# Part of the next expert's gate product moved between an expert's up and down products, token transposes moved into up, and three paddings

## The chip, the cores and the metric

The kernel runs on one core of a Trainium2 chip. The metric is the device time of one execution in microseconds. Lower is better.

## The reference, cut to what matters

One encoder layer: an adaLN-modulated norm, one input projection into an attention group and an mLSTM group, an output projection, and then a mixture of 16 experts in which each expert picks its own 128 of the 1024 tokens. The change lies in the experts, and its paddings also move operands of the two projections.

```python
aff = jax.nn.softmax((h @ w_router).astype(jnp.float32), axis=-1)
gates, idx = lax.top_k(jnp.swapaxes(aff, 1, 2), cap)          # cap = 128 tokens of each expert
xe = jax.vmap(lambda hb, ib: hb[ib])(h, idx)
hid = jax.nn.silu(jnp.einsum('becd,edf->becf', xe, w_gate)) * jnp.einsum('becd,edf->becf', xe, w_up)
ye = jnp.einsum('becf,efd->becd', hid, w_down) * gates[..., None]
out = segment_sum(ye at idx)                                   # added into the residual stream
```

D is 2048 and the hidden width of an expert is 1024, in float32: each expert reads 8 MiB of gate, 8 MiB of up and 8 MiB of down weights.

## The kernel before

Every float32 product is made of three matmuls of a reduced float32 type (`mm3`, L416 to L418): high by high, high by low and low by high, where `hi` is the rounded operand and `lo` the rest. One matmul is 128x128 by 128x512.

**Weights of the experts.** They come in 384 chunks of 1 MiB through a ring of 14 slots (plus a few lent ones at the start); `load_next` (L921) issues one DMA on SP's queue (L941), and is called when a chunk has been split. A chunk holds two k, where a k is 128 rows of contraction by 1024 columns. `chunk` (L1312) splits each k: ScalarE writes `ehi` (L1321, 4 buffers), VectorE writes `elo` (L1327, 3 buffers). A k feeds 6 matmuls: 3 into each of two banks. Gate, up and down have 16 k each, so 96 matmuls each; a chunk column `cc` is 512 rows, that is 4 k in two halves.

**One expert.** `prep(e+1)` (L1256) makes the one-hot matrix of the next expert's tokens (`oh`, VectorE), 16 small matmuls for indices and gates, and issues the gather of its tokens on POOL's queue (L1268); ScalarE then scales the gathered rows (L1280). `gate_up(e)` (L1332) runs gate into two `acc` banks and up into two others; ScalarE applies Silu into the tile `y` (L1355, one buffer), and after up VectorE multiplies (L1359). `hidden_T` (L1363) transposes the hidden rows on TensorE (L1369), ScalarE and VectorE split them into `hT` (L1372, L1373). `tokens_T(e+1)` (L1284) transposes the next expert's tokens: 4 quarters of 4 transposes (L1293), each followed by four scalings into `xtmp` (L1302) and a split into `xh` and `xl` (L1305, L1306); xh and xl have one buffer for each quarter. `down(e)` (L1378) runs two halves of 1024 columns, both in the same two `s` banks; after each half VectorE scales them into `y` (L1394), and at the end an indirect DMA on POOL's queue adds `y` into the output (L1396).

**Order.** Engines take instructions in the order in which a scheduler placed them at build time by its own timeline; `tc.issue_after` adds an order on one engine. In the order before, up of expert e ends, 8 token transposes, 8 hidden transposes and 8 more token transposes follow, and then down.

**PSUM.** Four `acc` banks, two `s`, two `t`.

**Places in SBUF.** Tiles are laid one after the other. In the layout before, `quad1`, `quad2` and `quad3` (pool `big`, the split activations of the projections, L184) begin 128 bytes past a multiple of 256, as `y` and `hT` do; the other quads and the split weights `w_hi` and `w_lo` (pool `wp`) begin at a multiple of 256; `xh`, `xl`, `ehi` and `elo` begin 192 bytes past one. In the input projection (`block_T` L425, `block_N` L456) the first half of the contraction reads quads 0 to 3, the second half quads 4 to 7; in the output projection (`out_block` L758) the stationary operand is always in quads 1 to 4.

Of the kernel before, what the change touches and what calls it, by code (L numbers as in the profile page):

```python
# [19 lines left out]
D = 2048  # L20
# [64 lines left out]
def tile_kernel(ctx: ExitStack, tc: tile.TileContext, x, c, w_ada, b_ada, w_in, b_gates, q_gain, k_gain, sink,  # L85
# [829 lines left out]
    ew = ctx.enter_context(tc.tile_pool(name="ew", bufs=8, side="right"))  # L915
    chunks, left, extra = {}, [], []

    def order(e, i):
        return MIXED if e + i // 4 == 0 else PLAIN

    def load_next(eng=nc.sync):  # L921

        n = len(chunks)
        if n == 16 * 24:
            return
        n, slot = FIRST[n] if n < len(FIRST) else (n, (n - len(FIRST)) % RING)
        i, half = divmod(n, 2)
        e, i = divmod(i, 12)
        if i < 8:
            cc, half = order(e, i)[2 * (i % 4) + half]  # L930
            i += cc - i % 4
            src, off, ld = (w_gate, w_up)[i // 4], e * D * 1024 + (i % 4) * 512 * 1024, 1024
        else:
            src, off, ld = w_down, e * 1024 * D + (i % 2) * 512 * D + ((i - 8) // 2) * 1024, D
# [242 lines left out]
    mo_p = ctx.enter_context(tc.tile_pool(name="moe", bufs=1))  # L1177
    borrowed(mo_p, "y")
    borrowed(mo_p, "hT")
    mo_p.tile([128, 8], F32, name="pad")  # L1180
    while len(chunks) < len(FIRST):
        load_next()
    todo, made = [0], [0]
# [97 lines left out]
        p.update(mt=mt, idx=idx, xg=xg)  # L1281
        yield

    def tokens_T(p, after=None):  # L1284
        p["xh"], p["xl"], p["tmp"] = [], [], []
        for q in range(4):
            xh = mo_p.tile([128, 4, 128], F32R, name=f"xh{q}")
            xl = mo_p.tile([128, 4, 128], F32R, name=f"xl{q}")
            ps = bank("t")
            tmp = mo_p.tile([128, 512], F32, name="xtmp", bufs=2)  # L1290
            with tc.issue_after(after.ins) if after else nullcontext():
                for b in range(4):
                    nc.tensor.transpose(ps[:, b * 128:(b + 1) * 128],  # L1293
                                        p["xg"][:, (4 * q + b) * 128:(4 * q + b + 1) * 128], ident)
            for b in range(4):
                k = 4 * q + b
                bs = slice(b * 128, (b + 1) * 128)
                if after is None and b % 2:
# [12 lines left out]

    def chunk(half, direct=False):  # L1312
            raw = chunks[todo[0]]
            todo[0] += 1
            for j in range(2):
                if direct:
                    yield 2 * half + j, raw[:, j], None
                    continue
                hi = mo_p.tile([128, 1024], F32R, name="ehi", bufs=4)
                lo = mo_p.tile([128, 1024], F32R, name="elo", bufs=NLO)  # L1320
                nc.scalar.copy(hi, raw[:, j])  # L1321
                n = made[0]
                made[0] += 1
                r = min(int((n - NLO) * PACES), len(chain) - 1)
                wait = P[0]["at"] if n < NLO else chain[r] if n < 48 else None
                with tc.issue_after(wait.ins) if wait else nullcontext():
                    nc.vector.tensor_sub(lo, raw[:, j], hi)  # L1327
                yield 2 * half + j, hi, lo
            if todo[0] - 1 not in lent:
                load_next()  # L1330

    def gate_up(e, p, side):  # L1332
        accs = []
        for w in range(2):
            acc = [bank("acc") for _ in range(2)]
            last = order(e, 4 * w)[-1]
            for cc, half in order(e, 4 * w):

                direct = e == 0 and (w, cc) in DIRECT
                for j, hi, lo in chunk(half, direct):  # L1340
                    k = 4 * cc + j
                    for q in range(2):
                        qs = slice(q * 512, (q + 1) * 512)
                        if direct:
                            p["last"] = nc.tensor.matmul(acc[q], p["tmp"][cc][:, j * 128:(j + 1) * 128], hi[:, qs],
                                                         start=k == 0, stop=(cc, half) == last and j % 2 == 1)
                            continue
                        p["last"] = mm3(acc[q], p["xh"][cc][:, j], p["xl"][cc][:, j], hi[:, qs], lo[:, qs],
                                        k == 0, (cc, half) == last and j % 2 == 1)
                    side.step()  # L1350
            if w == 0:
                yt = mo_p.tile([128, D], F32, name="y", tag="y")
                sg = [yt[:, q * 512:(q + 1) * 512] for q in range(2)]
                for q in range(2):
                    nc.scalar.activation(sg[q], acc[q], AF.Silu)  # L1355
        p["y"], p["hid"] = yt, []
        for q in range(2):
            hid = yt[:, 1024 + q * 512:1024 + (q + 1) * 512]
            nc.vector.tensor_mul(hid.rearrange("t (j p) -> t p j", j=4), acc[q].rearrange("t (p j) -> t p j", j=4),  # L1359
                                 sg[q].rearrange("t (p j) -> t p j", j=4))  # L1360
            p["hid"].append(hid)

    def hidden_T(p):  # L1363
# [11 lines left out]
            p["hl"].append(hl)  # L1375
            yield

    def down(p, side):  # L1378
# [4 lines left out]
        for half in range(2):  # L1383
            acc = [bank("s") for _ in range(2)]
            for cc in range(2):
                for j, hi, lo in (s for half in range(2) for s in chunk(half)):
                    for q in range(2):
                        qs = slice(q * 512, (q + 1) * 512)
                        mm3(acc[q], p["hh"][cc][:, j], p["hl"][cc][:, j], hi[:, qs], lo[:, qs],
                            cc + j == 0, cc == 1 and j == 3)  # L1390
                    side.step()
            for q in range(2):
                qs = slice(half * 1024 + q * 512, half * 1024 + (q + 1) * 512)
# [5 lines left out]
    P, g2b = [{} for _ in range(16)], []  # L1399
# [4 lines left out]
    first.add(tokens_T(P[0]))  # L1404
    first.drain()
    run(select(tp))
    for e in range(16):
        if e < 15:
            side.add(prep(e + 1, P[e + 1]))
        gate_up(e, P[e], side)  # L1410
        side.drain()
        if e + 1 < 16:
            side.add(tokens_T(P[e + 1], P[e]["last"]))
        ht = hidden_T(P[e])
        side.step()
        next(ht)
        side.step()
        next(ht)
        down(P[e], side)
        side.drain()  # L1420


# [43 lines left out]
```

## Time and profile before

| | |
|---|---|
| median of 3 runs | 2886.38 us (2884.27 to 2890.02) |
| the profiled execution | 2886.07 us, its span 2884.4 us |
| busy: TensorE / its weight loads / VectorE / ScalarE / GpSimd | 93% / 74% / 74% / 54% / 13% |
| mean granted TensorE clock | 0.976 |
| moved by DMA | 744.34 MB, 258 GB/s over the span |

The experts run from about 1620 us to the end. In a row of a view, PE is TensorE, PEld its weight loads, DVE VectorE, ACT ScalarE, POOL GpSimd and SP the engine whose queue loads the weights; L416 is line 416 of the kernel; out<-in names tiles. Matmuls are pipelined, and a row's duration is longer than the distance from one to the next: the pace is read from start times, or from a window divided by the number of matmuls that start in it.

### The profile page before, as it was taken

Reading aid. Unit: us, or ns where it says so; the run is one execution under the profiler, and the core shown is the slowest. Engines: PE = TensorE matmul, PEld = TensorE weight load, DVE = VectorE, ACT = ScalarE, POOL = GpSimd, SP = SyncE. Lnnn points to the kernel's source line nnn. Section 1 sums busy time; section 2 is a strip of 40 time slices with the busy share of each in tenths; the row PEclk is TensorE's granted clock in tenths of the full one; section 3 lists DMA queues with packets and bytes.
Section 4 is the critical chain, followed back from the end, with each engine's and each line's share of the span. In section 5 each row is a group of like instructions: output and inputs, shape, how many; then the busy total and the mean of one; then the engine's idle time right before and its main releaser. Section 6 shows DMA issues by size and latency. Waiting matters only on the chain. (4 is left out here: it accounts for less than half of the span.)

```text
span 2884.4 us, 36984 instructions
## 1 busy us (share of the span) xinstructions
PE 2669.0 (93%) x12384; PEld 2137.3 (74%) x12384; DVE 2127.7 (74%) x3504; ACT 1571.8 (54%) x2585; POOL 370.7 (13%) x306
## 2 busy tenths in 40 slices
PE   6997999999999999999999697999999999999997
PEld 6786787777777787777888476777777777777776
DVE  7777767766656556666646787988888888888886
ACT  5222432334333324333545376887788887777775
POOL 0001222000000003333435310010000000000000
PEclk9998999999999999999999799999999999999999
DMA  8874426655555556565786588999999999999993
GB/s 294 281 247 119 151 79 200 189 171 191 172 169 188 161 174 230 211 204 179 278 290 206 197 289 313 365 347 364 370 362 360 361 360 363 351 351 354 358 339 135
DMA packets 269399, 744.34 MB, mean 258 GB/s; under 512 B 29197, under 2 KB 83209, under 8 KB 232217
## 3 DMA queue, kind: packets, MB, share of 16 engines
q1 hardware_dynamic: 249240, 684.37, 66.2%
q0 software_dynamic: 4768, 33.62, 4.5%
q10 hardware_dynamic: 15200, 24.00, 2.3%
q8 instruction: 97, 1.59, 0.2%
q14 instruction: 94, 0.76, 0.1%
HBM read 672.01 MB, written 69.90 MB: 257 GB/s over the span
## 5 line engine op out<-in xcount | busy, mean ns | idle before, releaser
L1327 DVE TENSOR_TENSOR elo<-ew,ehi 128x1024 fp32r<-128x1024 f32 x432 | 513.2, 1221 | 68.4 <-ACT ehi L1321 19.9
L1321 ACT CAST ehi<-ew 128x1024 fp32r<-128x1024 f32 x432 | 445.1, 1055 | 134.9 <-PE acc L418 71.6
L1327 DVE TENSOR_TENSOR elo<-quad,ehi 128x1024 fp32r<-128x1024 f32 x324 | 384.3, 1221 | 65.1 <-ACT ehi L1321 32.8
L417 PE MATMUL acc<-elo,xh 128*128 128x512 f32 x1008 | 395.7, 393 | 4.1 <-DVE elo L1327 4.0
L418 PE MATMUL acc<-ehi,xl 128*128 128x512 f32 x1008 | 393.5, 391 | 0.0
L1321 ACT CAST ehi<-quad 128x1024 fp32r<-128x1024 f32 x324 | 333.2, 1055 | 101.0 <-PE acc L418 51.1
L416 PE MATMUL acc<-quad,w_hi 128*128 128x512 f32 x896 | 362.9, 406 | 7.2 <-ACT w_hi L385 5.0
L418 PE MATMUL acc<-quad,w_lo 128*128 128x512 f32 x896 | 358.1, 402 | 2.8 <-DVE w_lo L386 2.8
L417 PE MATMUL acc<-quad,w_hi 128*128 128x512 f32 x896 | 359.8, 402 | 0.0
L206 DVE SCALAR_TENSOR_TENSOR ada_acc<-ada_w,csil,ada_acc 128x512 f32<-128x512 f32 x360 | 273.4, 760 | 83.7 <-DMA ada_w<-in_w_ada_dram 80.1
L385 ACT ACTIVATE w_hi<-w_raw,sc1p 128x128 fp32r<-128x128 f32 (+2 forms) x368 | 161.7, 490 | 318.0 <-PE acc L417 175.8
L416 PE MATMUL acc<-ehi,xh 128*128 128x512 f32 x1008 | 314.1, 393 | 10.8 <-ACT ehi L1321 10.8
L417 PE MATMUL acc<-w_lo,quad 128*128 128x512 f32 x768 | 313.3, 408 | 6.7 <-DVE w_lo L375 5.2
L418 PE MATMUL acc<-w_hi,quad 128*128 128x512 f32 x768 | 308.0, 401 | 0.0
L416 PE MATMUL acc<-w_hi,quad 128*128 128x512 f32 x768 | 298.8, 417 | 9.0 <-ACT ev L728 4.6
L769 POOL TENSOR_TENSOR w_raw<-w_raw,quad 128x512 f32<-128x512 f32 x136 | 184.4, 1366 | 899.5 <-DMA quad<-mod_d 612.0
L416 PEld LDWEIGHTS acc<-ehi,xh 128*128 128x128 f32 x1008 | 189.9, 189 | 52.2 <-ACT ehi L1321 11.7
L417 PEld LDWEIGHTS acc<-elo,xh 128*128 128x128 f32 x1008 | 190.1, 189 | 50.4 <-DVE elo L1327 9.9
L386 DVE SCALAR_TENSOR_TENSOR w_lo<-w_raw,sc1p,w_hi 128x128 fp32r<-128x128 f32 (+2 forms) x368 | 174.0, 502 | 69.9 <-ACT w_hi L385 67.7
L417 PE MATMUL s<-elo,hT 128*128 128x512 f32 x512 | 208.2, 407 | 15.9 <-DVE elo L1327 15.6
L418 PEld LDWEIGHTS acc<-ehi,xl 128*128 128x128 f32 x1008 | 190.0, 188 | 39.1
L416 PE MATMUL s<-ehi,hT 128*128 128x512 f32 x512 | 181.3, 405 | 38.9 <-DVE y L1394 19.5
(377 smaller groups left out, 4158.1 us busy)
## 6 DMA issues: line engine op xcount, KB each, us to landing
ada_w<-in_w_ada_dram SPq DMA_DIRECT2D x192, 512.0 KB
ew<-in_w_down_dram SPq DMA_DIRECT2D x74, 1024.0 KB
ew<-in_w_up_dram SPq DMA_DIRECT2D x73, 1024.0 KB
ew<-in_w_gate_dram SPq DMA_DIRECT2D x72, 1024.0 KB
quad<-in_w_up_dram SPq DMA_DIRECT2D x54, 1024.0 KB
quad<-in_w_down_dram SPq DMA_DIRECT2D x54, 1024.0 KB
quad<-in_w_gate_dram SPq DMA_DIRECT2D x54, 1024.0 KB
w_raw<-in_w_in_dram SPq DMA_DIRECT2D x176, 256.0 KB
```

What stands on the lines that cost most here:

```text
L206: alu.scalar_tensor_tensor(acc, t[:, j], csil[:, k:k + 1], acc, op0=OP.mult, op1=OP.add)
L385: nc.scalar.mul(h, r, s)
L386: nc.vector.scalar_tensor_tensor(l, r, s, h, op0=OP.mult, op1=OP.subtract)
L416: nc.tensor.matmul(ps, ah, bh, start=start, stop=False)
L417: nc.tensor.matmul(ps, ah, bl, start=False, stop=False)
L418: return nc.tensor.matmul(ps, al, bh, start=False, stop=stop)
L769: nc.gpsimd.tensor_mul(raw[:, 0], raw[:, 0], g1b[:, nb * 512:(nb + 1) * 512])
L1321: nc.scalar.copy(hi, raw[:, j])
L1327: nc.vector.tensor_sub(lo, raw[:, j], hi)
```

## The change

Between up and down of experts 1 to 14 stand the first 512 rows of contraction (chunk column 0, two halves of two k) of the next expert's gate product: one half, then the hidden transposes and the last quarter of the token transposes, then the other half. The first three quarters of the token transposes stand inside up, each after the last use of the xh and xl that it overwrites. The second half of down uses `acc` banks in place of the `s` banks. The list `uses` gives the loads the new order of use. Expert 0 keeps the old order. Three paddings grow: 128 bytes in `consts`, 128 in `mixconsts`, 192 in the pool of the experts, so that all operands named above begin at a multiple of 256 bytes.

```diff
+    consts.tile([128, 32], F32, name="pad")
...
-    mc.tile([128, 8], F32, name="pad")
+    mc.tile([128, 40], F32, name="pad")
...
-    def order(e, i):
-        return MIXED if e + i // 4 == 0 else PLAIN
+    def order(e, w):
+        return MIXED if e + w == 0 else PLAIN
+    uses = []
+    for e in range(16):
+        uses += [(e, 0, cc, half) for cc, half in order(e, 0) if e < 2 or cc]
+        uses += [(e, 1, cc, half) for cc, half in order(e, 1)]
+        if 0 < e < 15:
+            uses += [(e + 1, 0, 0, half) for half in range(2)]
+        uses += [(e, 2 + part, cc, half) for part in range(2) for cc in range(2) for half in range(2)]
...
-    mo_p.tile([128, 8], F32, name="pad")
+    mo_p.tile([128, 56], F32, name="pad")
...
+    def rows(e, p, w, cc, half, side):
+        if w not in p["acc"]:
+            p["acc"][w] = [bank("acc") for _ in range(2)]
+        acc, (first, last) = p["acc"][w], (order(e, w)[0], order(e, w)[-1])
+        direct = e == 0 and (w, cc) in DIRECT
+        for j, hi, lo in chunk(e, w, cc, half, direct):
+            start, stop = (cc, half) == first and j % 2 == 0, (cc, half) == last and j % 2 == 1
+            for q in range(2):
...
+                p["last"] = mm3(acc[q], p["xh"][cc][:, j], p["xl"][cc][:, j], hi[:, qs], lo[:, qs], start, stop)
+            side.step()
+
+    def gated(p):
+        yt = p["y"] = mo_p.tile([128, D], F32, name="y", tag="y")
+        for q in range(2):
+            nc.scalar.activation(yt[:, q * 512:(q + 1) * 512], p["acc"][0][q], AF.Silu)
+
+    def hidden(p):
+        yt, p["hid"] = p["y"], []
...
-            acc = [bank("s") for _ in range(2)]
+            acc = [bank("acc" if part else "s") for _ in range(2)]
...
     for e in range(16):
...
+        p, nxt = P[e], P[e + 1] if e < 15 else None
+        if nxt:
+            side.add(prep(e + 1, nxt))
+        for cc, half in order(e, 0):
+            if e < 2 or cc:
+                rows(e, p, 0, cc, half, side)
+        gated(p)
...
         side.drain()
+        turn = tokens_T(nxt) if nxt else iter(())
+        for cc in range(4):
+            for half in range(2):
+                rows(e, p, 1, cc, half, side)
+                if half == 0 and cc and nxt:
+                    with tc.issue_after(used.ins):
+                        next(turn)
+            used = p["last"]
+        hidden(p)
+        ht = hidden_T(p)
+        if nxt:
+            mid = Filler()
+            mid.add(iter(()))
+            rows(e + 1, nxt, 0, 0, 0, mid)
+            with tc.issue_after(nxt["last"].ins):
+                next(ht)
+                next(ht)
+                next(turn)
+            rows(e + 1, nxt, 0, 0, 1, mid)
+        else:
+            next(ht)
+            next(ht)
+        down(e, p, side)
```

## Rows read from the trace of the kernel before

**Rows 1.** PE's waits from 1778 us on: us in total, times, longest.

```profile
PE s L416 <- DVE y L1394: 19.5, 15, 1.6
PE s L416 <- DVE hT L1373: 19.2, 15, 2.4
PE s L417 <- DVE elo L1327: 15.4, 16, 1.3
PE s L1369 <- DVE y L1359: 13.1, 16, 1.3
```

**Rows 2.** PE's timeline around expert 6's down: start us, us, instruction, [wait].

```profile
2158.94 1.03 PE L1293 MATMUL t<-ident,xg 128*128 128x128 f32 x8
2159.89 0.66 PE L1369 MATMUL s<-ident,y 128*128 128x128 f32 x4
2164.24 0.50 PE L416 MATMUL s<-ehi,hT 128*128 128x512 f32 x1 [0.55 <-DVE hT L1373]
2164.58 0.39 PE L417 MATMUL s<-elo,hT 128*128 128x512 f32 x1
...
2173.87 0.50 PE L417 MATMUL s<-elo,hT 128*128 128x512 f32 x1 [1.28 <-DVE elo L1327]
...
2179.16 0.47 PE L416 MATMUL s<-ehi,hT 128*128 128x512 f32 x1 [1.34 <-DVE y L1394]
```

**Rows 3.** Windows of experts 6 and 11: us, then PE PEld DVE ACT POOL, clock, DMA.

```profile
2158.71:2164.24 5.53, 3.59 (x26) 2.62 (x24) 3.86 (x6) 5.22 (x13) 0.00 (x0) 1.00 1.01 416
2164.24:2190.48 26.24, 23.61 (x114) 18.41 (x114) 23.16 (x27) 19.50 (x27) 1.14 (x1) 1.00 0.86 329
2190.48:2233.76 43.28, 43.28 (x192) 35.58 (x190) 39.19 (x34) 36.05 (x38) 2.30 (x1) 1.00 1.01 375
2536.02:2542.93 6.91, 3.51 (x26) 2.62 (x24) 4.96 (x6) 6.04 (x13) 0.00 (x0) 1.00 1.01 420
2542.93:2546.44 3.51, 3.50 (x9) 2.80 (x9) 1.75 (x3) 3.51 (x11) 0.00 (x0) 0.52 0.62 252
```

**Rows 4.** DVE's timeline at expert 6 and, last row, at expert 11.

```profile
2172.60 5.76 DVE L1327 TENSOR_TENSOR elo<-ew,ehi 128x1024 fp32r<-128x1024 f32 x5
...
2535.99 1.97 DVE L1359 TENSOR_TENSOR y<-acc,y 128x512 f32<-128x512 f32 x2 [1.21 <-PE acc L418]
```

**Rows 5.** ACT's timeline at expert 11.

```profile
2536.89 2.90 ACT L1302 ACTIVATE xtmp<-t,sh2x,sc2x 128x128 f32<-128x128 f32 x8 [2.11 <-PE t L1293]
```

**Rows 6.** Windows that hold matmuls alone: us, PE busy (count), clock, DMA.

```profile
182.24:201.69 19.45, 19.45 (x85) 1.00 0.72 242
202.14:218.24 16.10, 16.10 (x72) 1.00 0.64 198
1370.38:1383.20 12.82, 12.82 (x56) 1.00 0.69 247
2179.46:2189.31 9.85, 9.85 (x44) 1.00 0.99 383
```

**Rows 7.** Loads: DMA from 2139 to 2159 us; ACT's and SP's waits from 1778.

```profile
DMA packets 1691, 8.35 MB, mean 417 GB/s; under 512 B 127, under 2 KB 127, under 8 KB 1217
...
ACT ehi L1321 <- DMA ew<-in_w_down_dram: 1.5, 5, 0.3
...
SPq L941 <- DVE elo L1327: 895.4, 326, 10.3
```

**Rows 8.** Timelines of POOL, ACT and PE after expert 0; POOL at expert 6.

```profile
1720.87 2.43 POOL L1396 DMA_INDIRECT out_dram<-y,idx  x1 [22.83 <-PE acc L418]
1723.60 10.55 POOL L1268 DMA_INDIRECT xg<-x1p_d,idx  x1 [0.30 <-issue]
...
1746.15 1.22 PE L416 MATMUL acc<-ehi,xh 128*128 128x512 f32 x2 [10.50 <-ACT ehi L1321]
...
2171.79 1.14 POOL L1268 DMA_INDIRECT xg<-x1p_d,idx  x1 [51.98 <-ACT ehi L1321]
2193.27 2.30 POOL L1396 DMA_INDIRECT out_dram<-y,idx  x1 [20.34 <-DVE y L1394]
```

More of the change, by code (lines that the diff above doesn't have):

```diff
@@ L926, in load_next @@
         n, slot = FIRST[n] if n < len(FIRST) else (n, (n - len(FIRST)) % RING)
[L927 to L932, printed above, removed]
+        e, w, cc, half = uses[n]
+        if w < 2:
+            src, off, ld = (w_gate, w_up)[w], e * D * 1024 + cc * 512 * 1024, 1024
         else:
-            src, off, ld = w_down, e * 1024 * D + (i % 2) * 512 * D + ((i - 8) // 2) * 1024, D
+            src, off, ld = w_down, e * 1024 * D + cc * 512 * D + (w - 2) * 1024, D
         if slot < 8:
@@ L1282, in prep, with tokens_T @@
         yield
-    def tokens_T(p, after=None):
+    def tokens_T(p, after=None, first=False):
         p["xh"], p["xl"], p["tmp"] = [], [], []
@@ L1297, in tokens_T @@
                 bs = slice(b * 128, (b + 1) * 128)
-                if after is None and b % 2:
+                if first and b % 2:
                     nc.vector.tensor_scalar(tmp[:, bs], ps[:, bs], sc2x[:, k:k + 1], sh2x[:, k:k + 1],
@@ L1310, in tokens_T, with chunk @@
             yield
[L1312 to L1315, printed above, removed]
+    def chunk(e, w, cc, half, direct=False):
+        n0 = todo[0]
+        raw = chunks[n0]
+        assert uses[n0] == (e, w, cc, half)
+        todo[0] += 1
+        for j in range(2):
+            if direct:
+                yield 2 * half + j, raw[:, j], None
+                continue
+            hi = mo_p.tile([128, 1024], F32R, name="ehi", bufs=4)
+            lo = mo_p.tile([128, 1024], F32R, name="elo", bufs=NLO)
+            nc.scalar.copy(hi, raw[:, j])
+            n = made[0]
+            made[0] += 1
+            r = min(int((n - NLO) * PACES), len(chain) - 1)
+            wait = P[0]["at"] if n < NLO else chain[r] if n < 48 else None
+            with tc.issue_after(wait.ins) if wait else nullcontext():
+                nc.vector.tensor_sub(lo, raw[:, j], hi)
+            yield 2 * half + j, hi, lo
+        if n0 not in lent:
+            load_next()
@@ L1316, in chunk @@
+    def rows(e, p, w, cc, half, side):
[6 more added lines that the diff above has]
+            for q in range(2):
+                qs = slice(q * 512, (q + 1) * 512)
                 if direct:
-                    yield 2 * half + j, raw[:, j], None
+                    p["last"] = nc.tensor.matmul(acc[q], p["tmp"][cc][:, j * 128:(j + 1) * 128], hi[:, qs],
+                                                 start=start, stop=stop)
@@ L1318, in chunk @@
                     continue
[L1319 to L1356, printed above, removed]
@@ L1376, in hidden_T, with down @@
             yield
-    def down(p, side):
+    def down(e, p, side):
         y = p["y"]
@@ L1382, in down @@
             nc.sync.dma_start(g2b[0], view(mod_d, 3 * D, [[0, 128], [1, D]]))
-        for half in range(2):
-            acc = [bank("s") for _ in range(2)]
+        for part in range(2):
+            acc = [bank("acc" if part else "s") for _ in range(2)]
             for cc in range(2):
-                for j, hi, lo in (s for half in range(2) for s in chunk(half)):
+                for j, hi, lo in (t for half in range(2) for t in chunk(e, 2 + part, cc, half)):
                     for q in range(2):
                         qs = slice(q * 512, (q + 1) * 512)
-                        mm3(acc[q], p["hh"][cc][:, j], p["hl"][cc][:, j], hi[:, qs], lo[:, qs],
-                            cc + j == 0, cc == 1 and j == 3)
+                        p["last"] = mm3(acc[q], p["hh"][cc][:, j], p["hl"][cc][:, j], hi[:, qs], lo[:, qs],
+                                        cc + j == 0, cc == 1 and j == 3)
                     side.step()
             for q in range(2):
-                qs = slice(half * 1024 + q * 512, half * 1024 + (q + 1) * 512)
+                qs = slice(part * 1024 + q * 512, part * 1024 + (q + 1) * 512)
                 nc.vector.scalar_tensor_tensor(y[:, qs], acc[q], p["mt"][:, 9:10], g2b[0][:, qs],
@@ L1397, in down @@
                                      in_=y, in_offset=None, compute_op=OP.add)
-    P, g2b = [{} for _ in range(16)], []
+    P, g2b = [{"acc": {}} for _ in range(16)], []
     first, side = Filler(), Filler()
@@ L1403, in tile_kernel @@
     first.drain()
-    first.add(tokens_T(P[0]))
+    first.add(tokens_T(P[0], first=True))
     first.drain()
@@ L1407, in tile_kernel @@
     for e in range(16):
-        if e < 15:
-            side.add(prep(e + 1, P[e + 1]))
-        gate_up(e, P[e], side)
-        side.drain()
[L1412 to L1420, printed above, removed]
+        p, nxt = P[e], P[e + 1] if e < 15 else None
[5 more added lines that the diff above has]
+        gated(p)
+        if e == 0:
+            for cc, half in order(e, 1):
+                rows(e, p, 1, cc, half, side)
+            side.drain()
+            side.add(tokens_T(nxt, p["last"]))
+            hidden(p)
+            ht = hidden_T(p)
+            for _ in range(2):
+                side.step()
+                next(ht)
+            down(e, p, side)
+            side.drain()
+            continue
+        side.drain()
+        turn = tokens_T(nxt) if nxt else iter(())
+        for cc in range(4):
+            for half in range(2):
+                rows(e, p, 1, cc, half, side)
+                if half == 0 and cc and nxt:
+                    with tc.issue_after(used.ins):
+                        next(turn)
+            used = p["last"]
+        hidden(p)
+        ht = hidden_T(p)
+        if nxt:
[9 more added lines that the diff above has]
+            next(ht)
+            next(ht)
+        down(e, p, side)
 _INS = ["x", "c", "w_ada", "b_ada", "w_in", "b_gates", "q_gain", "k_gain", "sink", "m_gain", "w_out", "w_router",
```

5 lines of the change are left out of this document (3 added, 2 removed).

## The prediction, made before the changed kernel was run

> **What bounds the kernel now.** I read the page's busy shares first: TensorE is busy 93% of the span, VectorE 74%, ScalarE 54%. Then a table of windows through one expert: of expert 6's 75.05 us, gate and up take 43.28 us, in which PE is busy throughout, and the other 31.8 us are a transition (5.53) and down (26.24), in which it isn't [rows 3]. DVE is busy 66.2 of the 75 us and ACT 60.8. Last the waits of PE over the experts: four kinds make 67 us of idle time, and none of them is for a load [rows 1]; ACT waited at most 0.3 us for a chunk, and SP's queue waits for free slots (895 us), so the loads run ahead of the work [rows 7]. So PE in its order is the bound, first in the number and pace of its matmuls, then in waits at the seams between up, down and the next gate. All sums below are made against the profiled execution's 2886.07 us (span 2884.4), which is 0.3 us under the median of the runs.
>
> **The seam between up and down.** PE's token transposes begin at 2158.94 and down at 2164.24, 5.30 us apart [rows 2]. Eight transposes take 0.95 us, so the 24 there are 2.85 us of work; the other 2.45 us wait for VectorE's product and for the hT split. Nine experts (1 to 9) look so; in five (10 to 14) the transition is 6.91 us, 6.68 without the last matmul of up, and the wait 3.83 [rows 3]. In the changed order 12 matmuls (2.7 us) follow up at once, then the hidden transposes, then 12 more. VectorE's two products need 1.97 us [rows 4], under 2.7, and the hT split has the second 2.7 us. I let the whole wait go. The transposes remain, but in four groups instead of one; the first matmul after a group takes 0.34 us where one takes 0.23 [rows 2], so three more returns cost 0.33. Gain: 2.1 us in nine experts, 3.5 in five.
>
> **The clock.** In those five, the first nine matmuls of down take 3.51 us at a granted clock of 0.52, the lower level; at the pace of expert 6 (0.229) they would take 2.06 [rows 3, 6]. What came before is a transition with PE busy 3.5 of 6.9 us. Dense matmuls there should leave the clock up: 1.45 us each.
>
> **The middle and the start of down.** The second half of down waits for VectorE to empty the two `s` banks: 1.34 us at expert 6, 19.5 us in 15 times [rows 1, 2]. With `acc` banks it doesn't; with the return, 1.4 us in each of experts 1 to 15. Those banks are free by then: up's pair was read by the products before down began. Late in the same half PE waits 1.28 us for an elo, about 1.0 on average [rows 1, 2], because VectorE does products, split, four token splits and the one-hot work in one burst. Three of the four token splits move into up and 5.4 us of matmuls come between. I take back 0.8 of 1.0 (bounds 0 and 1.0).
>
> **What is added.** First, the matmuls between up and down need elo of their own k, and VectorE also has the products there. At expert 6 two elo are done before up ends, at expert 11 about one. An elo costs 1.15 us (5.76 for 5) [rows 4], so where one is missing it comes 1.97 + 1.15 = 3.1 us after up's end, while PE has 1.36 + 0.45 us to do: a wait of about 1.3. I take 0.4 us in the nine experts and 1.0 in the five; bounds 0 and 2.3 (no elo ahead). Behind such a wait stands all of PE's queue. Second, up gets three quarters of token transposes, with 2.90/2 = 1.45 us of xtmp on ACT each [rows 5] and an xh and xl. ACT is busy 36.05 and DVE 39.19 of gate and up's 43.28 us [rows 3], so 3 x 2.1 us on ACT and 3 x 0.7 on DVE just fit; I take 0.3 us (bounds 0 and 1.0). Third, Silu must wait until the scatter has left `y`, and gate after down is now 5.4 us shorter; but its result is first needed at up's end, 22 us later, so 0. The loads keep their number and lead; the gather still follows the last token transposes, which end at the same distance from up's end: 0.
>
> **The paddings.** In one block of the input projection, the first half of the contraction (quads 0 to 3, of which 1 to 3 begin at 128 past a multiple of 256) has 84 matmuls in 19.45 us, 231.5 ns each, and the second half (quads that begin at a multiple) 71 in 16.10, 226.8 ns: counts less the one still draining, same lines, same clock [rows 6]. The output projection, always with such a quad, runs 55 in 12.82, 233.1 ns. Down (hT at 128, ehi at 192) runs 43 in 9.85, 229.1 ns; gate and up (all at 192) 191 in 43.28, 226.6 [rows 3, 6]. So operands that agree in their place are at 226.7, others above it; the change makes all agree. Half of 14 x 192 matmuls by 4.7 ns is 6.3 us, half of 768 by 4.7 is 1.8, 1536 by 6.3 is 9.7: 17.8 us at most, 0 at least. I take 13, since part of those matmuls stand beside waits and transposes. In down 96 by 2.4 ns is 0.23 us an expert.
>
> The Trainium skill, "TensorE: Matmul & The Clock Gate", section "Part 2: What happens when you issue a matmul", says that PE reads its moving operand and its weights through two independent ports, so that loading the next weights does not slow the running matmul. By that rule where the operands lie would not matter; the two halves above, 231.5 against 226.8 ns, speak against it, and the rival below gives its time.
>
> **Sum.** Nine experts: 2.1 + 1.4 + 0.8 + 0.23 - 0.4 - 0.3 = 3.8; five: 3.5 + 1.45 + 1.4 + 0.8 + 0.23 - 1.0 - 0.3 = 6.1. That is 34.5 + 30.4; expert 15 gives 1.6, expert 0 (old order) 0.2: 67 us. With 13 from the projections, 80: 2886 - 80 = 2806 us. All terms at their better ends give 2786, at their worse ends 2864.
>
> **Rivals.**
>
> *The wait only moves (small gain).* If the order on VectorE puts the products ahead of both k in the middle, or the token quarters in up hold ACT's casts back, the added waits are 2.3 + 1.0 instead of 0.7 to 1.3: 2.3 us more in 14 experts, 33 us. Then 2839. For it: VectorE ran both products back to back at expert 11 [rows 4]. Against it: with three elo buffers VectorE has two k ready when up ends in most experts.
>
> *Places do not matter.* Then the 13 and 16 x 0.23 go: 2822. For it: the first half of the contraction could be slow from what else runs. Against it: the same difference in the output projection.
>
> *The loads take over.* A period falls from 75 to about 71 us. Of that, 24 chunks of 1.05 MB at the 417 GB/s of a stretch with loads alone are 60 us [rows 7], and the gather and the scatter come on top; they'd have to take over 11 us. If they do by 2 us an expert, 28 us go, of which the loads' lead pays part: about 2820 to 2834.
>
> The Trainium skill, "SBUF — State Buffer", section on a wrong bandwidth-pool intuition, gives about 358 GB/s between HBM and a core; an estimate by it is 70 us for the 25.2 MB alone, and the experts would gain almost nothing. The trace's 417 GB/s over 20 us speaks against it.
>
> *Slower: the gather behind the scatter.* After expert 0 the scatter went out at 1720.87 and the gather at 1723.60; ACT stood at the scaling of the gathered rows, its casts queued behind, and PE waited 10.5 us [rows 8]. From expert 1 on the gather goes 21 us ahead of the scatter (2171.79, 2193.27). It depends on PE slipping 16 small matmuls into a gap of down; the change fills those gaps. If the planner therefore puts them behind down, the gather falls behind the scatter, and 10.5 us in 13 experts are 137: 2886 - 80 + 137 = 2943. It decides as soon as more than 80/10.5, about 8, experts have it. Against it: token transposes still end early, and other gaps remain in the planner's timeline.
>
> **Chances.** Forecast 0.61; the wait only moves 0.16; places do not matter 0.07; loads 0.06; slower 0.10. This kernel's runs tell changes over 0.2% (5.8 us) apart from none. All but the last are faster: 0.87, with 0.03 for no change (several of the smaller gains together) and 0.10 for slower. Range 2776 to 2850: a little below the better ends, since further waits of gate in experts 1 to 4 may go too, and above to the rival whose wait moves. It leaves out the slower rival.
>
> **What would show it.** Right: PE's waits for `DVE y` (both lines) and for hT nearly gone; the distance between two experts at 70 to 71 us; the granted clock at full in every transition; first and second half of a projection block at the same 227 ns, and so the start of the experts about 13 us earlier. Wrong: PE waits for elo or ehi right after up that grow over 1.5 us an expert; ACT standing at the scaling of the gathered rows; ACT waiting for loads by microseconds; a scatter before the gather on POOL; the output projection still at 233 ns.

## The result, and the profile after

The changed kernel takes 2825.61 us (median of 4 runs, 2822.63 to 2829.70) against 2887.70 beside it: a ratio of 0.9777, 95% interval 0.9763 to 0.9791. The gain is 62 us by the medians and 64 by the ratio, where 80 were forecast. The profiled execution took 2826.7 us, with a span of 2824.9. The page first: PE's busy share, and the clock granted to it, by slices.

```profile
span 2824.9 us, 36954 instructions
PE 2654.1 (94%) x12384; PEld 2135.0 (76%) x12384; DVE 2115.1 (75%) x3504; ACT 1564.9 (55%) x2585; POOL 358.2 (13%) x306
...
PEclk9999999999999999999999889999999999999999
```

PE's waits over the experts, from 1778 us on (us in total, times, longest). Beside [rows 1] both waits for `y` are nearly gone, 13.1 to 1.0 ahead of the hidden transposes and 19.5 to 0 in the middle of down; hT has fallen from 19.2 to 6.7 and elo in down from 15.4 to 7.3. Two rows are new in size: elo for `acc`, that is in the gate rows and in up, and one single wait for ehi. All waits listed for this stretch make 26.3 us, before 74.5.

```profile
PE acc L418 <- DVE elo L1336: 7.7, 10, 2.2
PE s L418 <- DVE elo L1336: 7.3, 12, 1.1
PE s L417 <- DVE hT L1383: 6.7, 9, 0.8
PE acc L417 <- ACT ehi L1330: 2.9, 1, 2.9
PE s L1379 <- DVE y L1368: 1.0, 2, 0.7
PE s L417 <- ACT ehi L1330: 0.7, 1, 0.7
```

PE's timeline at expert 6, the answer to [rows 2]. Twelve matmuls of the next gate have run since up's end (from 2139.20, without a wait), then come the last four token transposes, the hidden transposes and twelve matmuls more (from 2143.52), and then PE stands again, for hT and for an elo. The last row is the middle of down: two matmuls without a wait, where there were 1.34 us.

```profile
2142.06 0.60 PE L1300 MATMUL t<-ident,xg 128*128 128x128 f32 x4
2142.49 0.34 PE L1269 MATMUL t<-place,oh 128*128 128x2 bf16 x8
2142.69 1.07 PE L1379 MATMUL s<-ident,y 128*128 128x128 f32 x8
2143.52 0.71 PE L417 MATMUL acc<-ehi,xh 128*128 128x512 f32 x2
...
2147.90 0.47 PE L417 MATMUL s<-ehi,hT 128*128 128x512 f32 x1 [0.84 <-DVE hT L1383]
2148.94 0.50 PE L418 MATMUL s<-elo,hT 128*128 128x512 f32 x1 [0.57 <-DVE elo L1336]
...
2158.75 0.62 PE L417 MATMUL acc<-ehi,hT 128*128 128x512 f32 x2
```

DVE at the same seam. Between the two halves of the hT split (L1383) stands the one-hot instruction of a later expert (L1265): the second half ends at 2147.75, and without that instruction's 1.21 us it would have ended at about 2146.6.

```profile
2140.28 2.03 DVE L1368 TENSOR_TENSOR y<-acc,y 128x512 f32<-128x512 f32 x2
...
2144.71 0.69 DVE L1383 TENSOR_TENSOR hT<-s,hT 128x512 fp32r<-128x512 f32 x1
2145.86 0.16 DVE L1281 TENSOR_REDUCE mt<-t 128x2 f32<-128x6 f32 x1 [0.46 <-PE t L1280]
2145.94 1.21 DVE L1265 TENSOR_TENSOR oh<-iot,slot 128x1024 bf16<-128x1024 f32 x1
2147.07 0.68 DVE L1383 TENSOR_TENSOR hT<-s,hT 128x512 fp32r<-128x512 f32 x1
```

Windows (us, then busy time of PE, PEld, DVE, ACT, POOL, clock, DMA share, GB/s): expert 6 from the hidden transposes to the next ones in three parts, and the first 5.3 us of expert 11's down. To be seen: the clock stands at 1.00 at expert 11, where [rows 3] have 0.52, and in the last part of expert 6 (the rest of the next gate, up, and the first added matmuls), DVE is busy for 38.87 of 44.83 us.

```profile
2142.69:2149.28 6.59, 5.19 (x38) 3.77 (x35) 6.05 (x10) 6.59 (x11) 0.98 (x1) 1.00 0.92 339
2149.28:2170.41 21.13, 21.13 (x94) 17.29 (x93) 19.90 (x20) 15.90 (x16) 0.00 (x0) 1.00 0.97 371
2170.41:2215.24 44.83, 44.17 (x206) 35.19 (x205) 38.87 (x37) 37.91 (x51) 2.30 (x1) 1.00 1.01 379
2504.73:2510.00 5.27, 3.86 (x16) 2.50 (x15) 5.27 (x7) 4.24 (x6) 0.00 (x0) 1.00 0.94 364
```

Windows that hold matmuls alone, the answer to [rows 6] (us, PE busy and count, clock, DMA): the first and the second half of the same block of the input projection, and a block of the output projection. Less the one still draining they run at 226.8, 227.0 and 227.1 ns, where they ran at 231.5, 226.8 and 233.1.

```profile
188.86:205.87 17.01, 17.01 (x76) 1.00 0.63 201
206.34:222.46 16.12, 16.12 (x72) 1.00 0.61 180
1371.15:1383.64 12.49, 12.49 (x56) 1.00 0.73 252
```

And yet the first expert matmul starts at 1638.2 us, where it started at 1638.7. From hidden transposes to hidden transposes, which is called a period below, the nine experts 4 to 12 take 645.6 us where they took 681.8: 71.7 against 75.8 each.

### The profile page after: what moved, and what is told of

It reads as the page before. It is cut to its first block, busy times and chain, and to the rows that moved or that the text cites. A ratio compares the mean times of both kernels' runs of the same rounds, so it can differ in the third digit from the quotient of the medians.

```text
span 2824.9 us, 36954 instructions
## 1 busy us (share of the span) xinstructions
PE 2654.1 (94%) x12384; PEld 2135.0 (76%) x12384; DVE 2115.1 (75%) x3504; ACT 1564.9 (55%) x2585; POOL 358.2 (13%) x306
## 5 line engine op out<-in xcount | busy, mean ns | idle before, releaser
L418 PE MATMUL acc<-elo,xh 128*128 128x512 f32 x1008 | 401.5, 398 | 10.2 <-DVE elo L1336 9.3
L417 PE MATMUL acc<-ehi,xh 128*128 128x512 f32 x1008 | 322.9, 399 | 13.8 <-ACT ehi L1330 13.8
L417 PE MATMUL acc<-w_hi,quad 128*128 128x512 f32 x768 | 297.4, 415 | 10.3 <-ACT ev L729 6.6
L396 DVE SCALAR_TENSOR_TENSOR accv<-w_raw,sh,accv 128x256 f32<-128x256 f32 (+1 forms) x210 | 116.9, 557 | 118.9 <-DMA w_raw<-in_w_in_dram 117.0
L417 PEld LDWEIGHTS acc<-quad,w_hi 128*128 128x128 f32 x896 | 172.6, 193 | 42.7 <-ACT w_hi L386 5.3
```

Source lines behind the costliest of these rows:

```text
L396: nc.vector.scalar_tensor_tensor(accv, raw[:, j], s, accv, op0=OP.mult, op1=OP.add)
L417: nc.tensor.matmul(ps, ah, bh, start=start, stop=False)
L418: nc.tensor.matmul(ps, ah, bl, start=False, stop=False)
```

## The experiments

All ratios are to the kernel before, run on the same chip in the same hours, with their 95% intervals; "gain" is what the ratio leaves of 2886 us. "Experts" is the time from the first expert matmul to the end of the profiled span, in one execution of each kernel.

| kernel | median us | ratio | gain us | experts us |
|---|---|---|---|---|
| before | 2884 to 2888 | 1 | 0 | 1245.7 |
| changed | 2825.61 | 0.9777 (0.9763 to 0.9791) | 64 | 1186.7 |
| places alone | 2877.55 | 0.9977 (0.9966 to 0.9988) | 7 | 1243.8 |
| order alone | 2831.44 | 0.9814 (0.9800 to 0.9827) | 54 | 1190.1 |
| changed, down in s | 2817.36 | 0.9759 (0.9745 to 0.9773) | 70 | 1182.4 |
| changed, no next rows | 2878.75 | 0.9972 (0.9961 to 0.9984) | 8 | 1245.0 |
| changed, tokens at the seam | 2837.68 | 0.9829 (0.9805 to 0.9852) | 49 | 1205.4 |
| changed, one-hot in down | 2814.01 | 0.9747 (0.9727 to 0.9766) | 73 | 1181.7 |
| changed, gather first | 2813.28 | 0.9747 (0.9728 to 0.9766) | 73 | 1178.4 |
| one-hot in down, gather first | 2804.17 | 0.9722 (0.9708 to 0.9736) | 80 | 1169.9 |
| the same, down in s | 2803.88 | 0.9729 (0.9710 to 0.9748) | 78 | 1173.0 |

### Places alone, and the order alone

```diff
 # the kernel before, and:
+    consts.tile([128, 32], F32, name="pad")
-    mc.tile([128, 8], F32, name="pad")
+    mc.tile([128, 40], F32, name="pad")
-    mo_p.tile([128, 8], F32, name="pad")
+    mo_p.tile([128, 56], F32, name="pad")
```

> The kernel before with the three paddings alone; the order of the work is untouched. If the projections' matmuls set the time of their stage, as the prediction took it: 13 us there, so the experts start 13 us earlier, and 0.23 us in each of 16 downs; 17 us in all, about 2870 us. If the projections wait for other work most of the time, so that faster matmuls only make the waits longer: the pace falls from about 232 to 228 ns in the first halves of the blocks all the same, the experts start 0 to 2 us earlier, and with 2 to 4 us in down the time is 2880 to 2886 us. If the paddings themselves slow some early block (T2's first half took 25.8 us after, 23.2 before): that block stands near 25.8 us here too.

Measured: 2877.55 us, 6.6 us less than before (3.2 to 9.8). The experts are 1.9 us shorter. T2, the third block of the input projection, is not slow in its first half here: 23.4 us, and between 22.8 and 26.5 in the nine profiles with the new places.

The other way round, the changed kernel with these three lines taken back:

> The changed kernel with the paddings taken back (8 columns twice, none in consts), so that the operands lie where they did before and only the order of the experts is new. By the prediction's terms it gains 67 us less 16 x 0.23: 2822 us, 17 us above a changed kernel that were at 2805; measured from the changed kernel's 2825.6 this theory says 2843. If the projections' gain is lost to waits, only down's pace and the last output blocks are given back: 2827 to 2831 us.

Measured: 2831.44 us. From the two ratios the places are worth 10.7 us there, give or take 6; from the medians 5.8. The first theory's 17 us lie outside both intervals. The second theory's 2 to 6 us reach into that of the first run (3.2 to 9.8) and are not excluded.

The profiles say something of where the difference to 17 went. From the first matmul of the input projection to the first of the experts I took every distance between the starts of two successive PE matmuls; up to 252 ns of it counts as the matmul's pace, the rest as wait.

| | profiles | pace us | waits us | sum us |
|---|---|---|---|---|
| old places | 2 | 1408.5, 1408.8 | 171.6, 168.0 | 1580.1, 1576.8 |
| new places, mean | 9 | 1400.1 (1398.1 to 1400.9) | 174.9 (168.3 to 180.2) | 1575.0 (1566.4 to 1578.5) |

The matmuls became 8.6 us faster on the mean, with a spread of 3, so the faster pace is there in every profile. The waits stand 5 us higher on the mean, but with a spread of 12 from execution to execution of the same projections and only two profiles with the old places: that they grew because of the places is not shown. The changed kernel's own profile is the one with the longest waits of all (180.2), and its first projection matmul comes 1.1 us later; hence its start of the experts only 0.5 us earlier.

### The place by itself

```python
for i, a in enumerate(places):          # weights at 0, 64, 128, 192
    for j, b in enumerate(places):      # moving operand
        ...                             # 96 matmuls 128x512 in this pair of places
```

> Matmuls alone, nothing of the reference: 16 groups of 96 matmuls of 128x512 with the weights at 0, 64, 128 and 192 bytes past a multiple of 256 and the moving operand at the same four places, first with all other engines idle, then with ScalarE casting, VectorE subtracting and loads running beside. If operands that agree in their place are faster, as the prediction read it: the four groups with equal places take 226 to 228 ns a matmul and the twelve others 229 to 233, quiet or busy. If the place only matters against the writes of the other engines: all 16 alike (within 1 ns) when quiet, spread only when busy. If a place at a multiple of 256 is what counts: the group 0/0 alone is fast.

The side work did not wait for its pass: casts, subtractions and loads ran beside the first pass and had ended by about 460 us, so the groups named "quiet" ran in company and those named "busy", from weights at 64 on, alone. The groups with the weights at 128 (c) are clear of that change. PE's groups by line: count, busy us, mean ns of one matmul with its drain.

```profile
L118 PE MATMUL quiet_wc_mb<-mbig,wbig 128*128 128x512 f32 x96 | 22.6, 394 | 0.0
L118 PE MATMUL busy_wc_mb<-mbig,wbig 128*128 128x512 f32 x96 | 22.6, 394 | 0.0
...
L118 PE MATMUL busy_wc_ma<-mbig,wbig 128*128 128x512 f32 x96 | 22.5, 394 | 0.0
...
L118 PE MATMUL quiet_wc_ma<-mbig,wbig 128*128 128x512 f32 x96 | 22.5, 394 | 0.0
L118 PE MATMUL quiet_wc_md<-mbig,wbig 128*128 128x512 f32 x96 | 22.2, 392 | 0.0
L118 PE MATMUL busy_wc_md<-mbig,wbig 128*128 128x512 f32 x96 | 22.2, 392 | 0.0
...
L118 PE MATMUL quiet_wc_mc<-mbig,wbig 128*128 128x512 f32 x96 | 21.9, 389 | 0.0
...
L118 PE MATMUL busy_wc_mc<-mbig,wbig 128*128 128x512 f32 x96 | 21.9, 389 | 0.0
```

Between starts one matmul takes 226.9 ns where the two places agree, 229.1 where the moving operand lies 64 bytes past the weights (modulo 256), 232.4 at 128 and 233.3 at 192. All 16 pairs follow this within 0.3 ns by the difference of the places alone (the first group after the start left out), with the other engines at work or alone. So the first theory holds, for this pattern of matmuls, each with a weight load of its own. The second and the third fall.

### Down in s

```diff
-            acc = [bank("acc" if part else "s") for _ in range(2)]
+            acc = [bank("s") for _ in range(2)]
```

> The changed kernel, but both halves of down accumulate in the two s banks, as before. By the prediction's term the second half waits for VectorE to empty them again, 1.4 us in each of 15 experts: 21 us, 2847 us, and PE waits for y at the second half by about 20 us in the trace. If VectorE and ScalarE are so close behind PE that a stall of PE only shortens its later waits for elo and ehi: half of it, about 2836 us.

Measured: 2817.36 us, not slower at all, against both theories; the intervals of the two kernels overlap. The wait is back at half its size (us in total, times, longest):

```profile
PE s L417 <- DVE y L1404: 10.7, 15, 0.9
```

Experts 4 to 12 are 0.64 us longer each. But the period that begins at expert 1 falls from 75.6 to 70.7 us and the one at expert 13 from 73.9 to 70.6. The second loses an elo wait of 2.23 us ahead of expert 14's hidden transposes and the lower clock behind it; the elo waits of the gate rows and up make 2.1 us in all where they made 7.7, so this much of the second theory, that other waits shorten, is seen. The first has its reason in the changed kernel's own trace: on POOL the scatter of expert 1 takes 10.27 us, and ScalarE stands 5.58 us at expert 2's Silu, which overwrites `y`, with its casts queued behind it. Both rows are of the changed kernel, POOL and ACT.

```profile
1812.44 10.27 POOL L1406 DMA_INDIRECT out_dram<-y,idx  x1 [24.00 <-DVE y L1404]
...
1833.60 1.09 ACT L1362 ACTIVATE y<-acc 128x512 f32<-128x512 f32 x2 [5.58 <-DMA out_dram<-y,idx]
```

With the s banks the scatter takes 2.33 us and Silu runs at once. Why one early scatter takes 9 to 10.3 us in most of these kernels (in the kernel before it is expert 2's, 10.26) stays open.

### No rows of the next gate between up and down

```diff
-            rows(e + 1, nxt, 0, 0, 0, mid)
-            with tc.issue_after(nxt["last"].ins):
+            with tc.issue_after(p["last"].ins):
                 next(ht)
                 next(ht)
                 next(turn)
-            rows(e + 1, nxt, 0, 0, 1, mid)
 # and gate's first 512 rows back in their place, in the loads' order too
```

> The changed kernel, but no row of the next expert's gate runs between up and down: the hidden transposes and the last token transposes follow up's end at once and PE waits there. By the prediction's terms 2.1 us in nine experts and 3.5 + 1.45 in five come back, less the added waits (0.4 and 1.0): 15 + 20 = 35 us, about 2861 us, and PE waits for VectorE's product (y) about 1.3 us per expert. If VectorE is what PE waits for on either side of the seam, the wait only changed its name (after, PE still stands 1.4 us at expert 5 and 6 once the hidden transposes are done): about 1 us an expert, 2840 us.

Measured: 2878.75 us, 53 us slower than the changed kernel and far beyond both theories: the whole gain is gone but for 8 us. PE's timeline at expert 12: the hT wait alone is 2.31 us, and behind it six matmuls start 0.42 us apart, not 0.23.

```profile
2616.31 0.66 PE L1377 MATMUL s<-ident,y 128*128 128x128 f32 x4 [0.35 <-DVE mt L1269]
2619.28 0.80 PE L417 MATMUL s<-ehi,hT 128*128 128x512 f32 x1 [2.31 <-DVE hT L1381]
2619.88 0.63 PE L418 MATMUL s<-elo,hT 128*128 128x512 f32 x1
2620.30 0.63 PE L419 MATMUL s<-ehi,hT 128*128 128x512 f32 x1
2620.73 0.63 PE L417 MATMUL s<-ehi,hT 128*128 128x512 f32 x1
```

The windows show the same: PE busy 1.65 of 3.71 us, and then a granted clock of 0.72 on the mean over 6 us.

```profile
2614.29:2618.00 3.71, 1.65 (x16) 1.15 (x16) 3.71 (x7) 3.71 (x8) 0.00 (x0) 1.00 0.96 362
2618.00:2624.00 6.00, 4.72 (x15) 3.82 (x16) 2.73 (x5) 1.01 (x3) 1.14 (x1) 0.72 0.77 277
```

Counted from 1776 us on, 131 matmuls follow each other at 400 to 480 ns, as at the lower clock, and lose 26 us; it is 33 and 6.7 us in the kernel before, 21 and 4.2 in the changed one. So of the 58 us by which the experts differ from the changed kernel's, 22 are the clock. Most of the rest is waits, 60 us against 26.3, hT alone 28.5 against 6.7. Moving the token transposes into up without filling the seam empties it: it leaves PE 12 transposes there where it had 24, and the granted clock falls to the lower level at the seam of every expert from 1 to 14.

### Tokens at the seam

```diff
-                if half == 0 and cc and nxt:
+                if half == 0 and cc == 3 and nxt:
 ...
-                next(turn)
+                for _ in range(3):
+                    next(turn)
```

> The changed kernel, but only the first quarter of the next expert's tokens is transposed during up; the other three follow the hidden transposes, between the two halves of the added gate rows. By the prediction's terms three token quarters then stand in the seam's burst on VectorE and ScalarE again (0.8 us of elo wait per expert, and ScalarE's 1.45 us per quarter ahead of the hT casts or of ehi): 1 to 3 us in each of 14 experts, 2840 to 2867 us. If the rows between up and down alone carry the gain: within 5 us of the changed kernel, 2821 to 2831 us.

Measured: 2837.68 us, some 12 to 15 us slower than the changed kernel, between the two. PE's waits for elo in down grow from 7.3 to 17.8 us, about 0.75 an expert, as the first theory's term has it; ScalarE's part of that theory is not seen, and the wait for hT falls from 6.7 to 0.5.

```profile
PE s L418 <- DVE elo L1336: 17.8, 14, 1.8
```

No theory named the clock. By the same count as above, less nine distances that hold a wait of 0.25 us, 68 matmuls run at the lower level here and lose 13.5 us, 21 and 4.2 in the changed kernel: 9 of the 18.7 us by which the experts differ. The added rows alone do not keep the clock up.

### The one-hot instruction, and the gather ahead of the scatter

```diff
+        with tc.issue_after(after.ins) if after else nullcontext():
             nc.vector.tensor_tensor(oh, ...)         # after: first y emptying of down(e - 2)
```

> The changed kernel, with VectorE's one-hot instruction of the expert after next queued behind the first emptying of down's banks instead of between the two halves of the hT split. At expert 6 of the changed kernel that instruction (1.21 us) sits between the halves and PE stands 0.84 us for hT and 0.57 us for an elo. If the seam's remaining wait comes from the order on VectorE: PE's waits for hT (6.7 us) and for elo at down's start (7.3 us) go down by 8 to 12 us together and the time by as much, 2814 to 2818 us. If VectorE has no slack anywhere (busy over 90% of an expert), the 1.2 us come back as a wait for elo in down: 2824 to 2828 us.

Measured: 2814.01 us, at the edge of the first theory's range; the intervals touch, but the trace shows the step. The hT wait is all but gone, elo in down is down from 7.3 to 4.6 us, and 2.5 us come back as elo waits in the gate rows and up. In the two profiles the experts are 5.0 us shorter; the rest of the difference of the medians lies in stages that the edit does not touch.

```profile
PE acc L418 <- DVE elo L1337: 10.2, 18, 2.2
PE s L418 <- DVE elo L1337: 4.6, 9, 0.5
...
PE s L417 <- DVE hT L1384: 0.8, 2, 0.4
```

```diff
-        nc.gpsimd.indirect_dma_start(out=out, ...)   # at the end of every down
+        if e:
+            scatter(p)
 ...
+                if e == 1 and (cc, half) == (0, 0):
+                    with tc.issue_after(nxt["fetch"].ins):
+                        scatter(P[0])
```

> The changed kernel, with expert 0's scatter queued behind expert 2's gather instead of ahead of it. If the 11.0 us for which PE stands at expert 1 come from the gather that follows the scatter on its queue (ScalarE waits 11.8 us for the gathered rows, its casts behind it): that wait goes and the time falls by 9 to 12 us, 2814 to 2817 us; the gather's instruction takes about 1.2 us on POOL instead of 10.5. If the gather is slow there by itself (data of expert 0's output still moving, or loads in the way): the wait stays, 2822 to 2829 us.

Measured: 2813.28 us. On POOL the gather now takes 1.11 us where it took 10.54 (10.55 in [rows 8]), and PE's wait for ehi at expert 1 falls from 11.0 to 3.1 us. The experts are 8.3 us shorter. The first theory holds, though not all of the wait goes: ScalarE still waits 4.63 us for the gathered rows.

```profile
1719.52 1.11 POOL L1275 DMA_INDIRECT xg<-x1p_d,idx  x1 [23.43 <-PE t L1280]
1720.94 7.34 POOL L1389 DMA_INDIRECT out_dram<-y,idx  x1 [0.30 <-issue]
```

### Both together

> The changed kernel with both single edits that helped: VectorE's one-hot instruction behind the first emptying of down's banks, and expert 0's scatter behind expert 2's gather. The two waits lie in different experts, so the gains should add: 8.7 + 8.9 from 2825.6 gives 2808 us (2805 to 2811). If the one-hot instruction's gain was partly taken at expert 1, where the other edit acts too: 2811 to 2814.

Measured: 2804.17 us (2803.51 to 2805.57), a little under the range stated. By the ratios 16 us are gained of the 17 of the two single edits, and the experts are 16.8 us shorter, where the single edits made them 5.0 and 8.3 shorter. The two gains add.

> The same with both halves of down in the s banks (the one-hot instruction behind the second emptying there). With the changed order alone that was 8 us faster, though PE waits about 0.7 us at each second half: expert 1 was 4.9 us shorter there, since its scatter took 2.3 us on POOL instead of 10.3 and Silu found y free, and expert 13 3.3 us shorter. If that is what it gained, and the s banks cost 0.6 us in each of some 11 experts: 2800 to 2806 us where expert 1 keeps its luck, 2812 to 2818 us where the scatter is short in the run with the acc banks too, that is slower than that run.

Measured: 2803.88 us, the same. The time lies in the first range, but its condition does not hold, so that is a hit by luck. Expert 1's scatter is long again (9.12 us, as in the run before; Silu waits 6.62 us for it where it waited 3.10, and the period is 77.9 us against 71.7), the period at expert 13 is 2.5 us shorter, experts 4 to 12 are 0.5 us longer each. So the gain at expert 1 was not the s banks', while the one at expert 13 came both times; and the acc banks in down's second half are worth nothing that can be measured.

### Fewer conditioning rows

```diff
         for j0 in range(0, 16, rows_at_once):
+            if j0:
+                yield None
+                continue
```

> The changed kernel with seven eighths of the conditioning product (the w_ada rows: their loads and VectorE's multiply-adds) left out, so its output is another; it is read against the next run, which differs from it in the places alone. In five profiles with the new places PE's matmul starts from the first projection to the first expert come 10 us nearer together, and the waits between them are 7 to 9 us longer than in two profiles with the old ones. If those waits are for the conditioning work that shares VectorE and the loads with the projections: without it the new places are worth their full 10 us there and 2 us in the experts, so this run is 10 to 14 us faster than the next. If the waits come back at whatever feeds the matmuls (ScalarE's and VectorE's halves of the weights): 3 to 8 us, as with the work in place (6.6 us with the places alone).

> The run before this one without the three paddings: the operands of the projections lie 128 bytes apart again. Seven eighths of the conditioning product are left out here too. 10 to 14 us slower than that run if the conditioning work took the gain back, 3 to 8 us if the feeding of the matmuls did.

Measured: 2792.07 us with the new places and 2797.53 with the old, 5.5 us apart by the medians and 6.6 us, give or take 6, by the ratios (0.9681, 0.9667 to 0.9695, and 0.9704, 0.9686 to 0.9721). Over the projections of the two profiles the pace is 1392.9 and 1402.7 us and the waits 152.1 and 151.1: in this pair the waits take 1 us back, not 5. The times lie in the second theory's range, and their interval reaches into the first one's; the waits of this one pair would fit the first. That the conditioning work is on the path is plain (without it the projections are 25 us shorter with the old places and 30 with the new, against the means above); whether it takes back a part of the places' gain is not settled.

## Why the forecast was right, and where it was off

**Direction and size.** Faster was forecast, 2806 us in a range of 2776 to 2850; it is 2826. The mechanism held, PE in its order and its waits at the seams. Of the 67 us for the experts 59 came; of the 13 for the projections 0.5 in the profiled execution and 3.5 on the mean of nine. That the experts' sum is so near is in part luck: taken back singly, by the prediction's terms the rows between up and down were worth 35 us and the banks 21, and the runs show 53 and nothing.

**The projections: the step that failed.** Its first half was right to the nanosecond: operands that agree in place run at 226.9 ns, others at 229 to 233, as [rows 6] had it. What failed is "I take 13, since part of those matmuls stand beside waits": only 8.6 us of pace were gained over the whole stage, and the stage became 3.5 us shorter on the mean. Whether the 5 us between went into waits that the faster matmuls lengthen, or are the scatter of the waits, stays open: places alone and order alone give 6.6 and 10.7 us for stage and experts together. [rows 6] are windows chosen for holding matmuls alone, and say nothing of how much of the stage is like them. The rival by which places do not matter had its time close (2822) and its reason wrong. The rule of the Trainium skill behind it ("TensorE: Matmul & The Clock Gate", section "Part 2: What happens when you issue a matmul"), by which a read port of its own keeps the load of the next weights from slowing the running matmul, does not foresee 233.3 against 226.9 ns with all other engines idle.

**The seam.** "I let the whole wait go" was too much: PE still stands 1.4 us at expert 6 and alike at 5, 7 to 9, 11 and 12, for hT and an elo (6.7 + 7.3 us in all). The wait for VectorE's product did go. The hT split did not fit into the second 2.7 us, because VectorE put the 1.2 us one-hot instruction between its halves; moved, the hT wait goes too. This is the rival "the wait only moves", in a milder form and mostly at another instruction than the two it named; its first, the products ahead of the elo, shows at experts 4 and 14 alone, with waits of 1.57 and 2.23 us.

**The clock.** 1.45 us in each of five experts was one window multiplied by a count: in the kernel before only the seams of experts 11, 13 and 14 stood at the lower level (0.51, 0.51 and 0.50 over 3.5 us), those of 10 and 12 at 1.00. Experts 10 and 13 of the kernel before:

```profile
2466.20:2469.80 3.60, 3.60 (x16) 2.97 (x17) 1.69 (x3) 3.60 (x11) 0.00 (x0) 1.00 0.49 203
...
2696.50:2700.00 3.50, 3.48 (x8) 2.80 (x9) 1.76 (x3) 3.50 (x11) 0.00 (x0) 0.51 0.56 232
```

The changed kernel has 11 and 13 at 1.00; at 14 PE waits 2.2 us for an elo behind the products, a case inside the bounds of 0 to 2.3, and the clock falls to a mean of 0.78 over 7.7 us, a window up to expert 14's hidden transposes:

```profile
2711.00:2718.70 7.70, 5.47 (x18) 4.00 (x17) 6.44 (x6) 2.93 (x4) 0.00 (x0) 0.78 0.91 351
```

By the count of slow matmuls the experts lose 4.2 us where they lost 6.7: 2.5 us came, of 7. Which seams fall differs between executions of one order: places alone, with the old order, loses 10.1 us, at experts 9 to 12, 14 and 15. What the working missed on the other side is what the clock would have cost without the rows between up and down: 26 us.

**The middle of down.** 1.4 us in each of 15 experts was mis-sized: the wait went, but given back it costs PE 0.7 us and a period 0.5 to 0.64, and the whole kernel nothing. About half of the wait thus goes with the new order alone; that VectorE empties the banks sooner because three token splits moved into up is likely, but not shown by itself. Part of what PE loses there it gets back as shorter elo waits.

**elo in down, and what is added.** 0.8 of 1.0 us an expert was forecast, 8 of 15.4 us came. Of the added waits, 0.4 to 1.0 us an expert at the seam and 0.3 in up, 12.8 us were forecast and 7.9 came: elo and ehi for `acc` make 10.6 us where they made 2.7. Only 3.8 of them stand at the seam, at experts 4 and 14.

**Silu.** "Its result is first needed 22 us later, so 0" is the one case costed at nothing that had a price: Silu's wait for `y` holds ScalarE's casts, and in expert 2 that cost PE 2.9 us, and the granted clock falls to its lower level behind it (0.83 on the mean from 1832 to 1842 us). The kernel before has a Silu wait of 2.6 us too, but PE does not wait behind it. What was queued behind the waiting instruction had to be counted.

**The loads and the gather.** Neither rival came. ScalarE waits 0.3 us for a chunk in all, and the gather goes 28 us ahead of the scatter at expert 6.

```profile
ACT ehi L1330 <- DMA ew<-in_w_down_dram: 0.3, 1, 0.3
...
2145.48 0.98 POOL L1275 DMA_INDIRECT xg<-x1p_d,idx  x1 [42.60 <-DVE hT L1383]
2173.11 2.30 POOL L1406 DMA_INDIRECT out_dram<-y,idx  x1 [26.65 <-DVE y L1404]
```

## What to carry to other kernels

A faster instruction in a stage is worth what the stage's waits leave of it: count pace and waits over the whole stage, in more than one execution, before multiplying a difference by a count. A seam that is filled with independent matmuls can gain twice, the wait and the clock behind it, and parts of such a change must not be priced one by one: the token transposes moved without the rows emptied the seam and were worth nothing, and the rows without the moved transposes lost 13.5 us to the clock. Before a wait is called gone, read what else the planner has put on the engine that ends it, as the one-hot instruction between the halves of the split.

## What was not expected of the hardware

The pace of back-to-back matmuls with a weight load each depends on the difference of the operands' addresses modulo 256 bytes: 226.9, 229.1, 232.4 and 233.3 ns for 0, 64, 128 and 192 bytes by which the moving operand lies past the weights, whether the other engines work or not. The same projections took between 1566.4 and 1578.5 us in nine executions, nearly all of it in the waits, so a single profile can't show a change of 4 us there. One or two of the scatters and gathers after the first experts take POOL 7 to 10.6 us; of the changed kernel's others the very first gather takes 4.07 and the rest 1 to 2.4.
